# Feed forward of a hybrid decoder layer: seven-product units from the eighth on, with weight sums and low parts moved from VectorE to GpSimd

## The chip, the cores and the metric

The kernel runs on one core of a Trainium2 chip. The metric is the device time of one execution in microseconds; every run named here is a whole execution of the layer.

## What is computed

One inference step of a decoder layer: a mixer (retention and dilated attention), then a SwiGLU feed forward, for a prompt of 512 tokens and 8 sample tokens together (520 columns). Only the feed forward is touched:

```python
def swiglu(xn, w_ffn_in, w_ffn_out):
    a, b = jnp.split(xn @ w_ffn_in, 2, axis=-1)
    return (jax.nn.silu(a) * b) @ w_ffn_out
...
h = h + swiglu(rmsnorm(h, ln2_g[layer]), w_ffn_in[layer], w_ffn_out[layer])
y = rmsnorm(h, lnf_g)
```

The model width is 1024 and the hidden width 2816, which is 22 tiles of 128 (NFF = 22). Everything is float32.

## The kernel before

Columns stand in two halves of 260 (256 prompt tokens and 4 sample tokens). To keep float32 precision each operand of TensorE is split into a high part, rounded by ScalarE, and a low part, which is the difference. A product is then three matmuls: high by high, high by low, low by high. Weights come from memory in subtiles of 128 x 1024 (`load_sub`, 512 KB each, four in flight), and are split in blocks of 128 x 512: `block_hi` (L201) on ScalarE writes `wh`, and two pumps later `low` (L204) on VectorE writes `wl`, five blocks ahead of TensorE (`AHEAD`).

The order is written out by hand. Engines take their instructions in program order. `advance(t)` is called as block t begins on TensorE: it issues the weight sums of blocks up to t + 6 and the high parts of blocks up to t + 5. `pump` is called after every second product of a block: it runs what `later(n, ...)` has put off and advances the generators by one `yield`.

The feed forward is a sequence of units (`FFSEQ`, L29). Unit i makes hidden tile i: a = silu(first product), times b. A plain unit (`ffn_in`) takes 2 x 8 products of 128 x 128 weights for two halves: 96 matmuls, 4 weight blocks. A quad (`ffn_in_quad`) computes the same four quarter results (two outputs by two halves) by the seven products of Winograd's form of Strassen's scheme (`SEVEN`, L284): 7 blocks of 4 x 3 matmuls, 84 in all, but 7 weight blocks, of which three hold sums of weights. `block_sum` makes these on VectorE: L185 two sums in one instruction of 1024 columns, L189 and L191 one each of 512. In a quad, ScalarE copies four of the seven results to SBUF (L313) and VectorE puts results together (`evac`: L1368, L1372, L1376). Two of the three PSUM banks of a quad belong to a pair that the next quad writes again from its first block on.

Output shares (`ffn_out`) are quads too. After a chunk of 8 units, four shares of two output columns each add the chunk's part to hT. Their right factors come from `right` (L1300): for each pair of units (4 tiles of 260 columns, `UF`) it makes four sums on VectorE, and the high parts of seven factors on ScalarE (UH) and their low parts on VectorE (L1318, UL), in three pieces of 780, 520 and 520 columns. It is a generator: pushed by `middle` after the odd unit of a pair, it runs over the pumps of the next unit. For the last chunk (units 16 to 21) `whole` splits each unit's result plainly, and plain products (`LAST` and the loops after it) end the kernel.

The sequence before is: units 0 to 8, four shares, units 9 to 16, four shares, units 17 to 21. Quads are 7, 8, 9, 11, 12, 13, 15, 16, 17, 19, 20, 21; units 10, 14 and 18 are plain. At the end `fin_out` scales the rows and SyncE stores them (L1475, L1477).

GpSimd has no part in the feed forward. Earlier in the kernel it adds the two gated branches (L1146) and sums of squares (L563).

Of the kernel before, what the change touches and what calls it, by code (L numbers as in the profile page):

```python
# [8 lines left out]
F32 = mybir.dt.float32  # L9
F32R = mybir.dt.float32r  # L10
AF = mybir.ActivationFunctionType
ALU = mybir.AluOpType
# [10 lines left out]
NFF = 22  # L23
# [1 line left out]
CHUNKS = ((0, 8), (8, 8), (16, 6))  # L25
LAST = [(c, k) for k0 in (0, 4) for c in range(2) for k in range(k0, min(k0 + 4, 6))]
LAST[8:] = [(0, 4), (1, 4), (0, 5), (1, 5)]
INQ = (7, 8, 9, 11, 12, 13, 15, 16, 17, 19, 20, 21)
FFSEQ = []  # L29
for (a_, n_), ahead_ in zip(CHUNKS, (1, 1, 0)):  # L30
    FFSEQ += [("in", i_, i_ in INQ) for i_ in range(a_ and a_ + 1, a_ + n_ + ahead_)]
    FFSEQ += [("out", c_, True) for c_ in range(0, 8, 2) if ahead_]
QUADS = {128 + 2 * i_: 4 for i_, e_ in enumerate(FFSEQ) if e_[2]}
SCW = (8, 7, 7, 6)
# [4 lines left out]
def tile_hybrid_layer(  # L39
# [9 lines left out]
    V, A, G_, PE, SP = nc.vector, nc.scalar, nc.gpsimd, nc.tensor, nc.sync  # L49
# [13 lines left out]
    def halves(ap):  # L63
        return ap.rearrange("p (f c) -> p f c", f=2)
# [10 lines left out]
    def f32(ap):  # L75
        return ap.bitcast(F32)
# [28 lines left out]
    def later(n, fn):  # L105
        delayed.append([n, fn])
# [31 lines left out]
    def push(name, gen):  # L138
        tracks[name].append(gen)
        return gen  # L140
# [9 lines left out]
    raw, split, qsum = {}, {}, {}  # L150
    blocks, bid = [], {}
    for s_ in range(NSUB):
# [3 lines left out]
        elif s_ - 1 not in QUADS:  # L156
            bid[s_, 0], bid[s_, 1] = len(blocks), len(blocks) + 1
            blocks += [("p", s_, 0), ("p", s_, 1)]
    done = {"add": 0, "hi": 0}
    home = []  # L160

    NRAW = 4
    AHEAD = 5

    def load_sub(s):
        if s < NSUB:
            raw[s] = wpool.tile([128, 1024], F32, tag="raw", bufs=NRAW, name=f"raw{s}")
            SP.dma_start(raw[s], wall[s])

    def left(b):  # L170
        kind, s, j = blocks[b]
        if kind == "p":
            return raw[s][:, 512 * j:512 * j + 512]
        w = 128 * QUADS[s]
        t, i = ((s, 1), ("q", 0), (s + 1, 0), (s + 1, 1), ("q", 1), ("q", 0), (s, 0))[j]
        return (qsum[s] if t == "q" else raw[t])[:, i * w:(i + 1) * w]

    def block_sum(b):
        kind, s, j = blocks[b]
        if kind == "p":  # L180
            return
        w = 128 * QUADS[s]
        if j == 1:
            qsum[s] = home[0].tile([128, 1024], F32, tag="qq", name=f"qq{s}")
            V.tensor_tensor(qsum[s][:, :2 * w].rearrange("p (i c) -> p i c", i=2),  # L185
                            raw[s][:, :2 * w].rearrange("p (i c) -> p i c", i=2),
                            raw[s + 1][:, :w][:, None, :].to_broadcast([128, 2, w]), op=ALU.add)
        elif j == 2:
            V.tensor_tensor(raw[s + 1][:, :w], raw[s][:, w:2 * w], qsum[s][:, :w], op=ALU.add)  # L189
        elif j == 5:  # L190
            V.tensor_tensor(qsum[s][:, :w], raw[s + 1][:, w:2 * w], raw[s + 1][:, :w], op=ALU.add)  # L191

    def block_tiles(b):
        w = 128 * QUADS[blocks[b][1]] if blocks[b][0] == "q" else 512
        split[b] = tuple(wpool.tile([128, 512], F32R, tag=t, bufs=6, name=f"{t}{b}")[:, :w] for t in ("wh", "wl"))
        return split[b]

    def block_hi(b):
        h, l = block_tiles(b)
        r = left(b)  # L200
        A.activation(h, r, AF.Copy)  # L201

        def low():
            V.tensor_tensor(l, r, f32(h), op=ALU.subtract)  # L204
            kind, s, j = blocks[b]
            if kind == "p" and j == 1:
                load_sub(s + NRAW)
            elif kind == "q" and j == 6:
                load_sub(s + NRAW)
                load_sub(s + 1 + NRAW)  # L210

        later(2, low)

    def advance(t):
        while done["add"] < min(t + AHEAD + 2, len(blocks)):
            b = done["add"]
            done["add"] += 1
            block_sum(b)
        while done["hi"] < min(t + AHEAD + 1, len(blocks)):
            b = done["hi"]  # L220
            done["hi"] += 1
            block_hi(b)
# [1045 lines left out]
    UF = {}  # L1268
    NP = CHUNKS[2][0]
    NX = 3  # L1270
# [4 lines left out]
    def whole(i, t):  # L1275
        hi, lo = (halves(u[:, i - NP, :]) for u in (UHp, ULp))
        A.activation(hi, t, AF.Copy)
        later(2, lambda: V.tensor_tensor(lo, t, f32(hi), op=ALU.subtract))

    def middle(i, mult):  # L1280

        if i > NP:
            t = halves(ftmp("fu"))
            mult(t)
            whole(i, t)
            return
        if i % 2 == 0:
            if len(rights) > 1:
                finish("S", rights[-2])
            UF[i // 2] = fp.tile([128, 4, HF], F32, tag="uf", bufs=2, name="uf")  # L1290
        t = UF[i // 2]
        mult(t[:, 1:3, :] if i % 2 else t[:, 0::3, :])
        if i == NX - 1:
            rights.append(push("S", right(UF[0], 0)))
        if i % 2 and i > NX - 1:
            rights.append(push("S", right(t, i % 8 // 2)))

    rights = []

    def right(b, k):  # L1300

        yield
        t = fp.tile([128, 4, HF], F32, tag="us", name="us")
        V.tensor_tensor(t[:, 0, :], b[:, 0, :], b[:, 3, :], op=ALU.subtract)
        yield
        V.scalar_tensor_tensor(t[:, 1, :], b[:, 2, :], -1.0, t[:, 0, :], op0=ALU.mult, op1=ALU.subtract)
        yield
        V.tensor_tensor(t[:, 2, :], b[:, 2, :], b[:, 3, :], op=ALU.subtract)
        yield
        V.scalar_tensor_tensor(t[:, 3, :], t[:, 1, :], -1.0, b[:, 1, :], op0=ALU.mult, op1=ALU.subtract)  # L1310
        yield
        for x, j, n in ((b[:, 0:3], 0, 3), (t[:, 0:2], 3, 2), (t[:, 2:4], 5, 2)):
            hi, lo = (u[:, k, j:j + n, :] for u in (UH4, UL4))
            A.activation(hi, x, AF.Copy)
            yield
            if k < 3:
                yield
            V.tensor_tensor(lo, x, f32(hi), op=ALU.subtract)  # L1318
            if k < 3:
                yield  # L1320

# [60 lines left out]
    def ffn_out(c):  # L1382

        s12, s35 = snaps()
        h1, h2 = halves(hT[:, c, :]), halves(hT[:, c + 1, :])

        def evac(j, bank):
            if j == 3:
                V.tensor_tensor(h1[:, 0, :], bank, h1[:, 0, :], op=ALU.add)
                later(1, lambda: V.tensor_tensor(h1, h1, s12, op=ALU.add))  # L1390
            elif j == 4:
                later(1, lambda: V.tensor_tensor(s35[:, 0, :], s35[:, 0, :], s35[:, 1, :], op=ALU.add))
            elif j == 5:
                V.tensor_tensor(h1[:, 1, :], bank, h1[:, 1, :], op=ALU.add)
                V.tensor_tensor(h2[:, 1, :], h2[:, 1, :], s35[:, 0, :], op=ALU.subtract)
            elif j == 6:
                V.tensor_tensor(h2[:, 0, :], h2[:, 0, :], bank, op=ALU.subtract)

        quad(ufactor, [s12[:, 0, :], s12[:, 1, :], s35[:, 0, :], s35[:, 1, :]], evac)

    for kind, i, seven in FFSEQ:
        if kind == "out":
            if i == 0:
                finish("S", rights[-1])
            ffn_out(i)
            continue
        if i == NP + 1:
            whole(NP, UF[NP // 2][:, 0::3, :])
        (ffn_in_quad if seven else ffn_in)(i)

    last = bpool.tile([128, 7 * D], F32, tag="bg", name="last")
    yt = last[:, :4 * D].rearrange("p (j c) -> p j c", j=4)
# [46 lines left out]
    def fin_out(f):  # L1459
        sq = ftmp("sqf")  # L1460
        A.activation(sq[:, :HF], hT[:, 7, f * HF:(f + 1) * HF], AF.Square)
        fin_ss(f, ssa[:, f * HF:(f + 1) * HF], True)
        a = fin_T(7, f)
        fin_ss(f, sq, False)
        r = rstd_rows(fp, ssb[:, 2 * f:2 * f + 2], 128, 2, D, "nf")
        r4 = rstd_rows(fp, ssb[:4, 4 + f:5 + f], 4, 1, D, "ng")
        fin_g(7, f, *a)
        for i in range(2):
            cs = slice(512 * i, 512 * i + 512)
            for j in (2 * f, 2 * f + 1):  # L1470
                if j % 2:
                    A.activation(yt[:, j, cs], yt[:, j, cs], AF.Copy, scale=r[:, 1:2])
                else:
                    V.tensor_scalar(yt[:, j, cs], yt[:, j, cs], r[:, 0:1], None, op0=ALU.mult)
                SP.dma_start(y_p[0, j * 128:(j + 1) * 128, cs], yt[:, j, cs])  # L1475
        V.tensor_scalar(ys[:, f, :], ys[:, f, :], r4[:4, 0:1], None, op0=ALU.mult)
        SP.dma_start(y_s[4 * f:4 * f + 4].rearrange("r o d -> r (o d)"), ys[:, f, :])  # L1477

# [26 lines left out]
    for f in range(2):  # L1505
        for c in range(4, 8):
            o = free_pair()[:, :1, :]
# [120 lines left out]
```

## Time and profile before

| | us |
|---|---|
| median of 3 runs | 1306.59 |
| lowest and highest of the runs | 1304.96, 1307.02 |
| the profiled execution's own time | 1305.23 |
| its span from first to last instruction | 1303.4 |

PE is TensorE, PEld its weight loads, DVE VectorE, ACT ScalarE, POOL GpSimd, SP SyncE. Times in the trace count from the start of the span. An instruction of VectorE is recorded from its own start, some 0.08 us before the one ahead of it ends, so the price of one in a row of them is the difference of two starts. Matmuls overlap in the records, so their price too is read from starts. Line numbers are those of the code above.

### The profile page before, as it was taken

The page shows a single profiled execution, that of the slowest core. Times are in us where ns is not written, and L with a number is a line of the kernel's source. Part 1 is how long each engine was busy: PE and PEld are TensorE (multiplying, and loading weights), DVE is VectorE, ACT ScalarE, POOL GpSimd, SP SyncE. Part 2 cuts the span into 40 slices and gives each one's busy share as a digit, 9 for nine tenths or more (in the row PEclk, how much of TensorE's full clock was granted, in tenths as well). Part 3 has the DMA queues.
Part 4 walks back from the last instruction along what each step waited for, and adds up shares of the span by engine and source line. Part 5 has one row for each costly group of instructions (what it writes and reads, how often), then busy time and mean ns, then how long its engine had stood idle before and what let it go on. Part 6 is the DMA issues. An engine that isn't in the chain of part 4 may idle for free.

```text
span 1303.4 us, 25688 instructions
## 1 busy us (share of the span) xinstructions
PE 1276.1 (98%) x10465; PEld 1245.0 (96%) x10465; DVE 821.0 (63%) x1737; ACT 573.5 (44%) x1100; POOL 83.6 (6%) x69
## 2 busy tenths in 40 slices
PE   8999999999999999999999999999999999999997
PEld 7999999999898999999999999899999999999997
DVE  7866636847765532234545455476688988798765
ACT  4465334635563522244434343233354555555542
POOL 3601001001002000000000000040000000000000
PEclk8999999999999999999999999999999999999999
DMA  6266344746584332435555545624222333233321
GB/s 213 93 208 230 119 158 140 250 153 230 171 292 149 98 95 84 138 122 159 159 150 157 160 149 189 222 98 147 82 82 82 98 112 100 87 93 113 98 82 66
DMA packets 89782, 183.35 MB, mean 141 GB/s; under 512 B 12024, under 2 KB 33944, under 8 KB 89664
## 3 DMA queue, kind: packets, MB, share of 16 engines
q1 hardware_dynamic: 88944, 180.64, 43.0%
q8 instruction: 82, 1.34, 0.4%
q10 hardware_dynamic: 720, 1.07, 0.3%
q14 instruction: 36, 0.29, 0.1%
HBM read 155.70 MB, written 25.98 MB: 139 GB/s over the span
## 4 chain that ended last, share of the span: by engine, by line
PE 85%; DVE 6%; DMA 3%; issue 2%; ACT 2%; POOL 1%; SPq 1%; DVEq 0%; ACTq 0%
PE pm L251 61%; PE pm L307 10%; PE sp L323 3%; PE pc L307 2%; PE sp L553 2%; DVE wl L204 2%; PE sp L572 1%; DMA vb<-vd 1%; PE pm L1516 1%; PE sp L968 1%; ACT wh L201 1%; PE sp L505 1%; DMA out<-st 1%; PE sp L918 1%; PE sacc L1113 1%
## 5 line engine op out<-in xcount | busy, mean ns | idle before, releaser
L251 PE MATMUL pm<-X,wh 128*128 128x260 f32 x3392 | 560.9, 287 | 4.4 <-DVE X L355 3.6
L251 PEld LDWEIGHTS pm<-X,wh 128*128 128x128 f32 x3392 | 469.5, 189 | 18.9 <-issue 9.1
L204 DVE TENSOR_TENSOR wl<-raw,wh 128x512 fp32r<-128x512 f32 x384 | 274.4, 716 | 165.0 <-ACT wh L201 161.6
L251 PE MATMUL pm<-X,wl 128*128 128x260 f32 x1696 | 342.3, 283 | 0.0
L201 ACT ACTIVATE wh<-raw 128x512 fp32r<-128x512 f32 x384 | 238.7, 625 | 210.7 <-PE pm L251 163.5
L251 PEld LDWEIGHTS pm<-X,wl 128*128 128x128 f32 x1696 | 262.5, 189 | 0.1
L251 PE MATMUL pm<-GA,wh 128*128 128x260 f32 x512 | 82.2, 283 | 0.0
L307 PE MATMUL pm<-XT,wh 128*128 128x260 f32 x384 | 71.5, 285 | 1.4 <-DVE uf L1376 1.2
L251 PE MATMUL pm<-XP,wh 128*128 128x260 f32 x448 | 71.9, 283 | 0.0
L251 PEld LDWEIGHTS pm<-GA,wh 128*128 128x128 f32 x512 | 70.1, 188 | 0.0
L307 PEld LDWEIGHTS pm<-XT,wh 128*128 128x128 f32 x384 | 59.1, 188 | 3.0 <-DVE uf L1376 2.0
L251 PEld LDWEIGHTS pm<-XP,wh 128*128 128x128 f32 x448 | 61.3, 188 | 0.0
L307 PE MATMUL pm<-UH,wh 128*128 128x260 f32 x192 | 54.6, 284 | 3.9 <-DVE fa L1368 2.8
L332 POOL TENSOR_TENSOR r<-v,cst 128x4 f32<-128x4 f32 (+4 forms) x14 | 17.6, 1261 | 598.0 <-DVE v L330 598.0
L307 PE MATMUL pm<-UH,wl 128*128 128x260 f32 x192 | 54.3, 283 | 0.0
L307 PE MATMUL pm<-UL,wh 128*128 128x260 f32 x192 | 54.3, 283 | 0.0
L307 PE MATMUL pm<-XT,wl 128*128 128x260 f32 x192 | 54.1, 282 | 0.0
L658 DVE SCALAR_TENSOR_TENSOR st<-st,kv 128x512 f32<-128x512 f32 x64 | 45.5, 714 | 13.3 <-ACT kv L623 11.5
L623 ACT ACTIVATE kv<-vb,ks 128x512 f32<-128x512 f32 x64 | 44.0, 714 | 22.0 <-DMA vb<-vd 20.8
L251 PE MATMUL pm<-GA,wl 128*128 128x260 f32 x256 | 51.6, 283 | 0.0
L313 ACT ACTIVATE s<-pm 128x260 f32<-128x260 f32 x80 | 30.9, 387 | 46.7 <-PE pm L307 46.4
L201 ACT ACTIVATE wh<-qq 128x512 fp32r<-128x512 f32 x60 | 37.0, 626 | 24.2 <-PE pm L251 11.6
(324 smaller groups left out, 2097.0 us busy)
## 6 DMA issues: line engine op xcount, KB each, us to landing
raw<-wall SPq DMA_DIRECT2D x192, 512.0 KB
st<-state SPq DMA_DIRECT2D x64, 256.0 KB
out<-st SPq DMA_DIRECT2D x64, 256.0 KB
area<-ck SPq DMA_DIRECT2D x24, 512.0 KB
vb<-vd SPq DMA_DIRECT2D x32, 256.0 KB
area<-qd SPq DMA_DIRECT2D x12, 512.0 KB
cb<-cd SPq DMA_DIRECT2D x4, 768.0 KB
xr<-xT SPq DMA_DIRECT2D x8, 260.0 KB
```

The source lines that it names most:

```text
L201: A.activation(h, r, AF.Copy)
L204: V.tensor_tensor(l, r, f32(h), op=ALU.subtract)
L251: PE.matmul(pm[:, f, :HF], w, x[f] if isinstance(x, tuple) else x[:, f * HF:(f + 1) * HF], start=first, stop=last)
L307: PE.matmul(out[bank], w[:, ks], factor(i, k, x), start=bank not in begun, stop=k == nkp - 1 and w is l, skip_group_check=True)
L313: A.activation(snap[(0, 3, 1, None, 2)[j]], out[bank], AF.Copy)
L323: PE.transpose(out, in_, ident[:n, :n])
L332: G_.tensor_tensor(r[:rows, :ncol], v[:rows, :ncol], mhalf[:rows].to_broadcast([rows, ncol]), op=ALU.pow)
L505: PE.matmul(sp[:, :T - i0], x[:, dt, jb * 128:(jb + 1) * 128], y[:, dt, i0:], start=i == 0, stop=i == len(mm) - 1)
L553: PE.matmul(sp[:, i0:], v[x][:, jb, c * 128:(c + 1) * 128], scs[y][:, SCO[jb]:SCO[jb] + T - i0], start=jb == 0 and x == y, stop=jb == 3 an ...
L572: PE.matmul(sp, kt[x][:, jb, dt * 128:(dt + 1) * 128], v[y][:, jb, :], start=jb == 0 and x == y, stop=jb == 3 and x == 1)
L623: A.activation(kvs[i][:, :DV], vbs[b], AF.Copy, scale=ks[:, dt, b:b + 1])
L658: V.scalar_tensor_tensor(sts[i], sts[i], GAMMA[h], kvs.pop(i)[:, :DV], op0=ALU.mult, op1=ALU.add)
```

## The change

`INQ` becomes all units from 7 on, and each run of output shares begins two units after its chunk's last unit instead of one: units 0 to 9, shares, 10 to 17, shares, 18 to 21. The first weight sum of a quad is made by GpSimd, two blocks earlier than before and into a tile of two buffers; VectorE makes the next two in place, block 2; GpSimd makes the fourth. The low parts in `right` are made by GpSimd. The `right` of the pair that was finished ahead of the shares (8 and 9) is pushed behind them, and so is `whole` for units 16 and 17. In the last `fin_out` the odd rows' stores are issued by ScalarE.

```diff
-INQ = (7, 8, 9, 11, 12, 13, 15, 16, 17, 19, 20, 21)
+INQ = tuple(range(7, NFF))
...
-    FFSEQ += [("in", i_, i_ in INQ) for i_ in range(a_ and a_ + 1, a_ + n_ + ahead_)]
+    FFSEQ += [("in", i_, i_ in INQ) for i_ in range(a_ and a_ + 2, min(a_ + n_ + 2, NFF))]
...
-        t, i = ((s, 1), ("q", 0), (s + 1, 0), (s + 1, 1), ("q", 1), ("q", 0), (s, 0))[j]
+        t, i = ((s, 1), ("q", 0), (s + 1, 0), (s + 1, 1), (s, 1), ("q", 0), (s, 0))[j]
...
+    def block_first_sum(b):
+
+        kind, s, j = blocks[b]
+        if kind == "q" and j == 0:
+            w = 128 * QUADS[s]
+            qsum[s] = home[0].tile([128, 512], F32, tag="qq", bufs=2, name=f"qq{s}")
+            G_.tensor_tensor(qsum[s][:, :w], raw[s][:, :w], raw[s + 1][:, :w], op=ALU.add)
...
-        if j == 1:
-            qsum[s] = home[0].tile([128, 1024], F32, tag="qq", name=f"qq{s}")
-            V.tensor_tensor(qsum[s][:, :2 * w].rearrange("p (i c) -> p i c", i=2),
-                            raw[s][:, :2 * w].rearrange("p (i c) -> p i c", i=2),
-                            raw[s + 1][:, :w][:, None, :].to_broadcast([128, 2, w]), op=ALU.add)
-        elif j == 2:
-            V.tensor_tensor(raw[s + 1][:, :w], raw[s][:, w:2 * w], qsum[s][:, :w], op=ALU.add)
-        elif j == 5:
-            V.tensor_tensor(qsum[s][:, :w], raw[s + 1][:, w:2 * w], raw[s + 1][:, :w], op=ALU.add)
+        if j == 2:
+            assert (s, 0) in lowered
+            V.tensor_tensor(raw[s][:, w:2 * w], raw[s][:, w:2 * w], raw[s + 1][:, :w], op=ALU.add)
+            V.tensor_tensor(raw[s + 1][:, :w], raw[s][:, :w], raw[s][:, w:2 * w], op=ALU.add)
+        elif j == 4:
+            assert (s, 1) in lowered
+            G_.tensor_tensor(qsum[s][:, :w], raw[s + 1][:, w:2 * w], raw[s + 1][:, :w], op=ALU.add)
...
+        while done["first"] < min(t + AHEAD + 4, len(blocks)):
+            b = done["first"]
+            done["first"] += 1
+            block_first_sum(b)
...
-        if i > NP:
+        if i > NP + 1:
...
-        if i % 2 and i > NX - 1:
+        if i % 2 and i > NX - 1 and i not in FIRSTS:
             rights.append(push("S", right(t, i % 8 // 2)))
...
+    FIRSTS = (9, 17)
...
-            V.tensor_tensor(lo, x, f32(hi), op=ALU.subtract)
+            G_.tensor_tensor(lo, x, f32(hi), op=ALU.subtract)
...
             ffn_out(i)
+            if i == 6:
+                o = FIRSTS[n_out]
+                n_out += 1
+                if o > NP:
+                    whole(NP, UF[NP // 2][:, 0::3, :])
+                    whole(NP + 1, UF[NP // 2][:, 1:3, :])
+                else:
+                    rights.append(push("S", right(UF[o // 2], 0)))
             continue
-        if i == NP + 1:
-            whole(NP, UF[NP // 2][:, 0::3, :])
...
-                SP.dma_start(y_p[0, j * 128:(j + 1) * 128, cs], yt[:, j, cs])
+                (A if f and j % 2 else SP).dma_start(y_p[0, j * 128:(j + 1) * 128, cs], yt[:, j, cs])
```

## Rows read from the trace of the kernel before

**Rows 1.** The page, part 1: busy time, share of the span, instructions of each engine.

```profile
PE 1276.1 (98%) x10465; PEld 1245.0 (96%) x10465; DVE 821.0 (63%) x1737; ACT 573.5 (44%) x1100; POOL 83.6 (6%) x69
```

**Rows 2.** The chain of waits in order of time: start us, us, what.

```profile
1006.44 4.31 PE pm L307 x36
...
1035.07 8.65 PE pm L307 x72
...
1045.16 8.65 PE pm L307 x72
...
1079.73 11.49 PE pm L251 x96
...
1124.16 11.49 PE pm L251 x96
...
1135.64 4.31 PE pm L307 x36
...
1208.94 11.49 PE pm L251 x96
```

**Rows 3.** The waits of TensorE from 880 us on: total us, times, longest.

```profile
PE pm L307 <- DVE fa L1368: 3.6, 3, 1.4
PE pm L307 <- DVE uf L1376: 2.3, 3, 1.2
```

**Rows 4.** The timeline of VectorE in unit 12: start us, us, instruction [idle before].

```profile
1105.27 1.22 DVE L185 TENSOR_TENSOR qq<-raw,raw 128x1024 f32<-128x1024 f32 x1
1106.40 0.43 DVE L1310 SCALAR_TENSOR_TENSOR us<-us,uf 128x260 f32<-128x260 f32 x1
...
1107.35 0.68 DVE L189 TENSOR_TENSOR raw<-raw,qq 128x512 f32<-128x512 f32 x1
1107.95 0.68 DVE L204 TENSOR_TENSOR wl<-qq,wh 128x512 fp32r<-128x512 f32 x1
1108.55 0.96 DVE L1318 TENSOR_TENSOR UL<-uf,UH 128x780 fp32r<-128x780 f32 x1
1109.43 0.42 DVE L1368 TENSOR_TENSOR fa<-pc,s 128x260 f32<-128x260 f32 x1
...
1111.92 0.42 DVE L1368 TENSOR_TENSOR fa<-pm,s 128x260 f32<-128x260 f32 x1
1112.26 0.68 DVE L191 TENSOR_TENSOR qq<-raw 128x512 f32<-128x512 f32 x1
1113.57 0.69 DVE L204 TENSOR_TENSOR wl<-qq,wh 128x512 fp32r<-128x512 f32 x1 [0.63 <-ACT wh L201]
1114.18 0.69 DVE L1318 TENSOR_TENSOR UL<-us,UH 128x520 fp32r<-128x520 f32 x1
1114.79 0.42 DVE L1376 SCALAR_TENSOR_TENSOR uf<-pm,fa 128x260 f32<-128x260 f32 x1
```

**Rows 5.** The timelines of VectorE (three rows) and GpSimd (one) after 859 us.

```profile
859.67 0.69 DVE L1148 TENSOR_TENSOR M<-sgat,M 128x520 fp32r<-128x520 f32 x1
860.28 1.80 DVE L204 TENSOR_TENSOR wl<-raw,wh 128x512 fp32r<-128x512 f32 x1
862.01 0.68 DVE L1145 TENSOR_TENSOR sgbt<-sgbt,pm 128x520 f32<-128x520 f32 x1
...
859.84 1.70 POOL L1146 TENSOR_TENSOR sgat<-sgat,sgbt 128x520 f32<-128x520 f32 x1 [1.17 <-DVE sgbt L1145]
```

**Rows 6.** The timelines of VectorE and GpSimd after 301 us, one row each.

```profile
301.15 0.75 DVE L564 SCALAR_TENSOR_TENSOR GT<-sp,vec,g 128x512 f32<-128x512 f32 x1 [2.60 <-ACT sq L562]
...
301.26 1.30 POOL L563 TENSOR_TENSOR ssa<-ssa,sq 128x512 f32<-128x512 f32 x1 [2.06 <-ACT sq L562]
```

**Rows 7.** Windows: stretch, length, busy us of PE, PEld, DVE, ACT, POOL, clock, DMA.

```profile
1091.20:1101.40 10.20, 10.20 (x88) 10.20 (x87) 8.00 (x13) 5.71 (x12) 0.00 (x0) 1.00 0.20 63
1030.50:1070.80 40.30, 40.30 (x335) 40.30 (x336) 37.06 (x66) 21.63 (x43) 0.00 (x0) 1.00 0.32 102
```

**Rows 8.** The timeline of SyncE's queue at the end.

```profile
1298.03 1.81 SPq L1475 DMA_DIRECT2D out<-last  x4
```

More of the change, by code (lines that the diff above doesn't have):

```diff
@@ L158, in tile_hybrid_layer @@
             blocks += [("p", s_, 0), ("p", s_, 1)]
-    done = {"add": 0, "hi": 0}
+    done = {"first": 0, "add": 0, "hi": 0}
     home = []
@@ L174, in left @@
         w = 128 * QUADS[s]
-        t, i = ((s, 1), ("q", 0), (s + 1, 0), (s + 1, 1), ("q", 1), ("q", 0), (s, 0))[j]
+        t, i = ((s, 1), ("q", 0), (s + 1, 0), (s + 1, 1), (s, 1), ("q", 0), (s, 0))[j]
         return (qsum[s] if t == "q" else raw[t])[:, i * w:(i + 1) * w]
+    lowered = set()
+    def block_first_sum(b):
[4 more added lines that the diff above has]
+            G_.tensor_tensor(qsum[s][:, :w], raw[s][:, :w], raw[s + 1][:, :w], op=ALU.add)
     def block_sum(b):
@@ L205, in low @@
             kind, s, j = blocks[b]
+            lowered.add((s, j))
             if kind == "p" and j == 1:
@@ L1399, in ffn_out @@
         quad(ufactor, [s12[:, 0, :], s12[:, 1, :], s35[:, 0, :], s35[:, 1, :]], evac)
+    n_out = 0
     for kind, i, seven in FFSEQ:
```

## The prediction

> **What bounds the kernel now.** I read the page first: TensorE is busy for 98% of the span, VectorE for 63%, GpSimd for 6% [rows 1]. So a microsecond is won only by giving TensorE less to do or by removing the places where it waits. Next, the chain of waits gives the length of the pieces. A plain feed-forward unit (96 products) takes 11.49 us, and an output share of seven products, 84 of them, takes 1045.16 - 1035.07 = 10.09 us when nothing holds it [rows 2]. The same rows show where TensorE is held. From 1006.44 to 1079.73 lie seven quads (units 7 and 8, four output shares, unit 9): 73.29 us against 7 x 10.09 = 70.63, so 2.66 lost. From 1135.64 to 1208.94 lie seven more (15, 16, four shares, 17): 2.67 lost. Units 11, 12 and 13 run from 1079.73 + 11.49 = 1091.22 to 1124.16, 32.94 against 30.27: 2.67 lost. Together 8.0 us. The waits of TensorE name the releaser: VectorE's additions of L1368 and its products of L1376, three times each [rows 3]. Both empty a bank that the next block writes.
>
> VectorE's timeline in unit 12 says why [rows 4]. A generator `right` makes seven right factors from each pair of units; it advances one step per pump, and a quad has 14 pumps, so all of it falls into the even unit that follows the pair. Starts of neighbours give the true price of one instruction: 0.60 us for 512 columns (1107.35 to 1107.95), 0.61 for 520 (1114.18 to 1114.79), 0.88 for 780 (1108.55 to 1109.43), 0.34 for 260 (1111.92 to 1112.26), 1.13 for 1024 (1105.27 to 1106.40). VectorE's work in an even quad is 7 low parts, 4.20; sums 1.13 + 0.60 + 0.60 = 2.33; five emptyings of 260, 1.70; `right` 4 x 0.34 + 0.88 + 2 x 0.61 = 3.46. That is 11.69 us against 10.09. The odd quad, without `right`, is 8.23. Units 10, 14 and 18 are plain now, and two of them absorb a `right`; units 8, 12 and 16 do not, and lose 2.67 each.
>
> **The change, part by part.**
>
> (a) Units 10, 14 and 18 become quads: 3 x (11.49 - 10.09) = 4.2 us less on TensorE, and that is on the path.
>
> (b) Weight sums. VectorE loses the 1024-wide sum and one of 512 and gains one of 512: -1.13 us per quad. GpSimd gets two of 512.
>
> (c) Low parts of the right factors: VectorE loses 0.88 + 0.61 + 0.61 = 2.10 per pair; GpSimd gets 780 and twice 520 columns.
>
> Without contention, (b) and (c) would settle the matter: the even quad would ask 8.46 us of VectorE and every wait would go. But the trace shows what a GpSimd addition does beside VectorE [rows 5]. GpSimd's addition of 520 columns begins at 859.84. VectorE finishes M, and its next instruction, a low part with two operands in SBUF, takes 1.80 us instead of 0.69. From the start of M to the start after the low part VectorE spends 862.01 - 859.67 = 2.34, of which 0.61 and 0.60 are its own: 1.13 us went to GpSimd. The pattern repeats for every M. By contrast an instruction of VectorE that takes one operand from PSUM runs beside a GpSimd addition undelayed, 0.75 us [rows 6]. So I price a GpSimd addition of 512 or 520 columns at 1.13 us of VectorE, and 780 columns in proportion at 1.70; it is hidden where VectorE is idle or works from PSUM. GpSimd's own record says 1.70 us for the 520 [rows 5]; if the whole of it blocked, a pair would lose another 4 us.
> The Trainium skill bears on that choice: Perfetto Trace Analysis, section GPSIMD Engine Instruction, says that a GpSimd span in a profile is not to be trusted and that spacing of starts is the better measure. By that rule, too, the smaller price stands.
> No row shows GpSimd writing the rounded type that `right` needs. VectorE's own price does not depend on it (sum and low part are both 0.60 in [rows 4]), so I take none; the bound above is the 1.70 of the record, below it is no block at all.
>
> Now unit by unit. An even quad up to its second L1368 loses 1.13 - 0.60 = 0.53 of sums and two low parts, 0.88 + 0.61 = 1.49: 2.02 less. In that stretch GpSimd runs the 780 low part, the fourth sum of the next quad and the first sum of the one after: 1.70 + 1.13 + 1.13 = 3.96 more. Of this I take 0.8 as hidden: VectorE has one idle place of 0.63 [rows 4], and one instruction in six reads PSUM, five chances at 0.34/6 each, 0.3. So VectorE reaches that point 1.1 later. Behind it the sum of L191 (0.60) and a low part (0.61) fall away, and one GpSimd low part (1.13) comes in: -0.1. An even quad then loses 2.67 + 1.0 = 3.7 us. The third low part slips into the odd quad, where VectorE is busy 8.00 us now [rows 7]: 8.00 - 1.13 + 3 x 1.13 = 10.3 at worst, nothing lost to speak of.
>
> Even quads with a `right` beside them were three and are five: 8, 10, 12, 14, 16. So 5 x 3.7 = 18.5 lost, where 8.0 were: +10.5.
>
> (d) Output shares two units later. A `right` no longer ends just ahead of them; it still ends in an even quad, so the wait moves from the start of the shares to units 8 and 16 and is in the five. In a share VectorE is busy 37.06/4 = 9.27 us [rows 7]; 9.27 - 1.13 + 2.26 = 10.4 less up to 1.0 for three instructions that read PSUM: 9.4 to 10.4 against 10.09. I take nothing; the upper end is 8 x 0.3 = 2.4.
>
> (e) `right` of units 8 and 9 starts after the shares, in unit 10; `whole` of 16 and 17 in unit 18, 2 x 0.61 of VectorE in a quad without `right`: nothing. The first weight sum is issued two blocks earlier and may wait for its weights at the head of GpSimd's queue; behind it stand only low parts that no block needs soon.
>
> (f) At the end two of five stores are issued by ScalarE, not SyncE, whose four row stores take 1.81 us in a row [rows 8]. The bytes are the same; the first is issued as before. Between -0.5 and +0.3; I take 0.
>
> Sum: -4.2 + 10.5 = +6.3. The profiled execution took 1305.2 us (span 1303.4), so it would take 1311.5. The median of the runs is 1306.6, 1.4 above it, and I carry the difference over: **1313 us**. Differences under 0.2% (2.6 us) are what a measurement of this kernel cannot tell from none.
>
> **The rivals.**
>
> *GpSimd fits into VectorE's gaps (faster).* If only the 780 low part and one sum meet VectorE before the emptying, the stretch is 1.70 + 1.13 - 0.8 - 2.02 = 0 later, and behind it 1.2 is saved with nothing coming in: an even quad loses 1.5, five lose 7.5, and the result is -0.5 - 4.2 = -4.7: 1302. For it: VectorE is idle 2.2 us of the odd quad [rows 7], and GpSimd is free to run when its operands are there. Against: GpSimd was started by the very stretch of VectorE work it collides with in [rows 5]. Without any contention all 8.0 would go, 1294.4; the trace speaks against that in every repetition. The Trainium skill (SBUF — State Buffer, section Who interferes with whom) frees only those instructions of VectorE that take at most one input from SBUF; [rows 6] agrees, and by that rule this rival would need most of VectorE's work to come from PSUM, which it does not.
>
> *A draw.* Even quads at 2.0 to 3.0 us: 10 to 15 lost, so -2.2 to +2.8: 1304.4 to 1309.4.
>
> *GpSimd becomes the bound (slower still).* Place: the in-place sum of block 2, which VectorE may write only after GpSimd has read the same columns for its first sum. GpSimd has 1.70 + 4 x 1.13 = 6.2 us of blocked time per even quad, by its record 4 x 1.70 and half as much again for the 780, 9.4 of 10.09. It decides once GpSimd is a block (1.44) behind: then VectorE stands still with the emptyings queued behind the sum. All five additions ahead of the emptying would give 1.70 + 4 x 1.13 - 0.8 - 2.02 - 1.2 = 2.2 more per even quad, 4.9 lost, 24.5 in all, and with 2.4 in the shares: +16.5 + 2.4 - 4.2 = +14.7, 1321.
>
> **How the numbers follow.** My forecast, 1309.5 to 1317, has 0.45; GpSimd as the bound 0.12; a draw 0.20; faster 0.23. Left out of the range are the unblocked case and the worst of the backlog: 1302 to 1320. Slower by over 0.2% is 0.57. The forecast's own range is 1309.5 to 1317.
>
> **What the profile would show.** Right: TensorE with 36 products fewer; GpSimd with some 6 us of additions per even quad; many low parts of VectorE at 1.2 to 1.8 us instead of 0.69 in units 7 to 21; TensorE's waits behind L1368 and L1376 once for each of units 8, 10, 12, 14, 16, some 3 to 4 us each, and none at the first output share. Wrong: low parts that stay at 0.69 beside GpSimd, waits of TensorE below 9 us in total, or waits that end on GpSimd rather than VectorE.

## The result and the profile after

The change is slower: 1356.76 us, median of 4 runs (1354.37 to 1359.3), against 1305.78 us of the kernel before on the same chip (1302.91 to 1307.02): ratio 1.0394, 95% interval 1.0366 to 1.0422. The profiled execution took 1354.37 us with a span of 1352.6, that is 49.2 more than the span before.

The page of the changed kernel, part 1, beside [rows 1]:

```profile
PE 1283.2 (95%) x10429; PEld 1243.8 (92%) x10429; DVE 866.6 (64%) x1720; ACT 580.0 (43%) x1121; POOL 197.2 (15%) x139
```

TensorE has its 36 instructions fewer. VectorE has 17 instructions fewer and is 45.6 us longer busy.

Line numbers from here on are those of the kernel that is being read. In the changed kernel L320 is L307 of the kernel before, L326 is L313, L209 is L201, L212 is L204, L1382 is L1368 and L1390 is L1376; L1408 adds a PSUM result to hT in a share.

The waits of TensorE from 1000 us on, beside [rows 3] (line waited for: total us, times, longest):

```profile
PE pm L320 <- DVE fa L1382: 22.0, 13, 3.2
PE pm L320 <- DVE hT L1408: 12.4, 8, 1.6
PE pm L320 <- DVE uf L1390: 5.3, 10, 0.6
PE pm L320 <- ACT s L326: 5.0, 5, 1.3
PE pm L320 <- DVE fu L1390: 1.6, 3, 0.6
```

Before there were six such waits, 5.9 us, all behind units. Now there are 39, 46.3 us. Every output share (`hT`, eight times) and every unit from 7 on but the last has one. In the waits of all engines from 1000 to 1300 us GpSimd is not named once as the one waited for.

The chain of waits of the changed kernel in order of time (start us, us, what), three shares and then the fourth blocks of units 10, 12 and 14, beside [rows 2]:

```profile
1060.67 4.59 PE pm L320 x36
...
1072.57 4.59 PE pm L320 x36
...
1084.46 4.59 PE pm L320 x36
...
1115.62 1.43 PE pc L320 x12
...
1142.72 1.43 PE pc L320 x12
...
1169.81 1.43 PE pc L320 x12
```

A share takes 11.9 us instead of 10.09, a pair of units 27.1 instead of 2 x 10.09 = 20.2.

The timeline of VectorE in one share (start us, us, instruction, idle time before it), then GpSimd's:

```profile
1075.30 0.69 DVE L212 TENSOR_TENSOR wl<-raw,wh 128x512 fp32r<-128x512 f32 x1 [0.91 <-ACT wh L209]
1076.68 0.69 DVE L212 TENSOR_TENSOR wl<-raw,wh 128x512 fp32r<-128x512 f32 x1 [0.70 <-ACT wh L209]
...
1079.42 0.42 DVE L1403 TENSOR_TENSOR hT<-pc,hT 128x260 f32<-128x260 f32 x1
1079.88 1.55 DVE L1404 TENSOR_TENSOR hT<-hT,s 128x520 f32<-128x520 f32 x1
1081.35 1.77 DVE L212 TENSOR_TENSOR wl<-raw,wh 128x512 fp32r<-128x512 f32 x1
1083.05 0.41 DVE L1406 TENSOR_TENSOR s<-s 128x260 f32<-128x260 f32 x1
1083.39 0.68 DVE L212 TENSOR_TENSOR wl<-raw,wh 128x512 fp32r<-128x512 f32 x1
1083.99 0.42 DVE L1408 TENSOR_TENSOR hT<-pm,hT 128x260 f32<-128x260 f32 x1
```

```profile
1079.58 1.29 POOL L199 TENSOR_TENSOR qq<-raw 128x512 f32<-128x512 f32 x1 [8.90 <-DVE wl L212]
1080.82 1.75 POOL L186 TENSOR_TENSOR qq<-raw,raw 128x512 f32<-128x512 f32 x1
```

GpSimd idles 8.9 us, until the low part of block 1 is made. Then it runs the fourth sum and right behind it the first sum of the quad after next. VectorE alternates with it: L1404 takes 1.55 us (0.70 unblocked, in the kernel with fills below), the low part 1.77 (0.69 unblocked). Some 2 us later than it would have, VectorE reaches L1408, the emptying of a bank that TensorE waits for. Some 4 us earlier VectorE had stood idle for 0.91 and 0.70 us.

The same two timelines in unit 12, an even unit with a `right`:

```profile
1128.20 2.32 DVE L195 TENSOR_TENSOR raw<-raw,raw 128x512 f32<-128x512 f32 x1
...
1132.18 1.64 DVE L212 TENSOR_TENSOR wl<-raw,wh 128x512 fp32r<-128x512 f32 x1
1133.74 1.53 DVE L1386 TENSOR_TENSOR s<-s 128x260 f32<-128x260 f32 x1
1135.20 1.74 DVE L212 TENSOR_TENSOR wl<-raw,wh 128x512 fp32r<-128x512 f32 x1
1136.86 0.42 DVE L1382 TENSOR_TENSOR fa<-pm,s 128x260 f32<-128x260 f32 x1
```

```profile
1128.09 1.89 POOL L1332 TENSOR_TENSOR UL<-uf,UH 128x780 fp32r<-128x780 f32 x1 [7.04 <-ACT UH L1328]
1132.01 1.26 POOL L199 TENSOR_TENSOR qq<-raw 128x512 f32<-128x512 f32 x1 [2.03 <-DVE wl L212]
1133.23 1.75 POOL L1332 TENSOR_TENSOR UL<-us,UH 128x520 fp32r<-128x520 f32 x1
1134.95 1.45 POOL L186 TENSOR_TENSOR qq<-raw,raw 128x512 f32<-128x512 f32 x1
```

Four additions of GpSimd stand ahead of L1382, and each meets a VectorE instruction: 1.63 us on L195 (2.32 against 0.69), then 0.95 on a low part, 1.1 on L1386 and 1.05 on the next low part.

### The profile page after: what moved, and what is told of

The parts are those of the page before. It is cut to its first block, busy times and chain, and to the rows that moved or that the text cites. A ratio compares the mean times of both kernels' runs of the same rounds, so it can differ in the third digit from the quotient of the medians.

```text
span 1352.6 us, 25785 instructions
## 1 busy us (share of the span) xinstructions
PE 1283.2 (95%) x10429; PEld 1243.8 (92%) x10429; DVE 866.6 (64%) x1720; ACT 580.0 (43%) x1121; POOL 197.2 (15%) x139
## 4 chain that ended last, share of the span: by engine, by line
PE 75%; DVE 13%; issue 5%; DMA 4%; ACT 2%; POOL 1%; SPq 1%; ACTq 0%; DVEq 0%
PE pm L264 53%; PE pm L320 9%; DVE wl L212 4%; PE sp L336 3%; PE sp L566 2%; PE pc L320 2%; DMA vb<-vd 2%; DVE s L1386 1%; PE sp L585 1%; PE pm L1537 1%; PE sp L981 1%; DMA out<-st 1%; DVE raw L195 1%; ACT wh L209 1%; PE sp L518 1%
## 5 line engine op out<-in xcount | busy, mean ns | idle before, releaser
L212 DVE TENSOR_TENSOR wl<-raw,wh 128x512 fp32r<-128x512 f32 x407 | 321.4, 792 | 178.5 <-ACT wh L209 176.7
L209 ACT ACTIVATE wh<-raw 128x512 fp32r<-128x512 f32 x407 | 253.0, 625 | 227.6 <-PE pm L264 153.1
L320 PE MATMUL pm<-XT,wh 128*128 128x260 f32 x480 | 92.9, 292 | 11.3 <-ACT s L326 5.0
L320 PEld LDWEIGHTS pm<-XT,wh 128*128 128x128 f32 x480 | 75.9, 194 | 15.6 <-ACT s L326 7.0
L320 PE MATMUL pm<-XP,wh 128*128 128x260 f32 x240 | 47.2, 295 | 23.4 <-DVE fa L1382 20.3
L320 PE MATMUL pm<-XT,wl 128*128 128x260 f32 x240 | 68.7, 286 | 0.0
L320 PE MATMUL pm<-UH,wh 128*128 128x260 f32 x192 | 55.2, 287 | 12.0 <-DVE hT L1408 9.3
L326 ACT ACTIVATE s<-pm 128x260 f32<-128x260 f32 x92 | 35.4, 385 | 62.9 <-PE pm L320 59.0
L320 PEld LDWEIGHTS pm<-XP,wh 128*128 128x128 f32 x240 | 37.8, 193 | 26.2 <-DVE fa L1382 22.6
L320 PE MATMUL pm<-UL,wh 128*128 128x260 f32 x192 | 54.3, 283 | 0.0
L320 PE MATMUL pm<-UH,wl 128*128 128x260 f32 x192 | 54.3, 283 | 0.0
L199 POOL TENSOR_TENSOR qq<-raw 128x512 f32<-128x512 f32 x23 | 29.8, 1296 | 153.5 <-DVE wl L212 153.5
```

What stands on the lines that cost most here:

```text
L199: G_.tensor_tensor(qsum[s][:, :w], raw[s + 1][:, w:2 * w], raw[s + 1][:, :w], op=ALU.add)
L320: PE.matmul(out[bank], w[:, ks], factor(i, k, x), start=bank not in begun, stop=k == nkp - 1 and w is l, skip_group_check=True)
L326: A.activation(snap[(0, 3, 1, None, 2)[j]], out[bank], AF.Copy)
```

## The experiments

Two things had to be told apart: whether GpSimd's additions cause the loss at all or the new order of the units does, and, if they do, whether it is how much they block or where the block falls. The period of a share is read from one row per kernel: all instructions of the last subtraction of a share (L1397 before, L1411 in the change) in the first four shares, with the first and the last start; their distance is three periods. The rows of the kernel before and of the change:

```profile
L1397 DVE TENSOR_TENSOR hT<-hT,pm x4: 418/419/419, 1040.0 to 1070.3; 128x260 f32<-128x260 f32 x4
```

```profile
L1411 DVE TENSOR_TENSOR hT<-hT,pm x4: 410/412/414, 1061.5 to 1097.2; 128x260 f32<-128x260 f32 x4
```

They give 10.1 and 11.9 us. Each kernel was timed beside the kernel before, whose medians on the chips used were 1302.8 to 1305.8 us; the ratios take that out, a difference between the medians of two experiments does not. Where units are named below, the period is the distance of the first matmuls of neighbouring quads' fourth blocks (`pc`) in the timeline. Before, an even quad so measured takes 12.55 us and an odd one 10.33; in the change 14.7 to 17.8 and 12.1.

**All on VectorE.**

```diff
-G_.tensor_tensor(qsum[s][:, :w], raw[s][:, :w], raw[s + 1][:, :w], op=ALU.add)
+V.tensor_tensor(qsum[s][:, :w], raw[s][:, :w], raw[s + 1][:, :w], op=ALU.add)
...
-G_.tensor_tensor(qsum[s][:, :w], raw[s + 1][:, w:2 * w], raw[s + 1][:, :w], op=ALU.add)
+V.tensor_tensor(qsum[s][:, :w], raw[s + 1][:, w:2 * w], raw[s + 1][:, :w], op=ALU.add)
...
-G_.tensor_tensor(lo, x, f32(hi), op=ALU.subtract)
+V.tensor_tensor(lo, x, f32(hi), op=ALU.subtract)
...
-while done["first"] < min(t + AHEAD + 4, len(blocks)):
+while done["first"] < min(t + AHEAD + 1, len(blocks)):
```

> The changed kernel with every weight sum and low part back on VectorE; the order of the units, all seven-product units from 7 on and the later shares stay. (The first sum is issued three blocks later than in the change, where the kernel before had it, and into one buffer.) Theory A, GpSimd's additions block VectorE: with none of them output shares come back to 10.1 us and odd units to 10.1 to 10.4 us; VectorE still has 11.7 us of work in each of the five even units, so these stay at some 12.7 us: 1297 to 1312 us in all. Theory B, it is the new order and the lack of plain units that overloads VectorE, whoever adds: shares and odd units stay near 12 us and the total is over 1335 us.

Measured: 1318.37 us, ratio 1.0104 (1.0089 to 1.0119). Shares 10.5 us, odd units 10.55, even units 13.2 to 14.5.

```profile
L1411 DVE TENSOR_TENSOR hT<-hT,pm x4: 415/416/417, 1052.4 to 1083.9; 128x260 f32<-128x260 f32 x4
```

VectorE with 70 additions more to do is faster than VectorE with GpSimd's help: 38 us of the 51 go. Theory B falls. The total is 6 us over the top of the expectation; the kernel with the old sums, below, shows where that comes from.

**The low parts alone, and the sums alone, on GpSimd.** The first kernel keeps `G_` in the low parts' line only, the second in the two sums' lines only (there with the change's own lead and buffers).

> As the first kernel of this set, but the low parts of the right factors are GpSimd's, as in the change; all weight sums are VectorE's. Theory A: shares at 10.1 us and odd units near 10.3 us, since no GpSimd work falls there; even units at 13 to 14.5 us, the two with the dense generator at 14 to 16 us; total 1310 to 1325 us. Theory B: over 1335 us.

> The changed kernel with only the low parts of the right factors back on VectorE; the two weight sums stay with GpSimd. Theory A: the two sums start together as soon as the low part of block 1 is ready, always between the third and the last but one emptying, and put that emptying off by two blocks of 1.1 us: shares stay at 11.9 us, odd units at 12.1 us, even units at 13.5 to 15 us; total 1335 to 1348 us, so that most of the loss is the sums' and not the low parts'. Theory C, it is the amount of blocked time that counts, wherever it falls: shares, where VectorE has the least work, near 10.1 to 10.4 us, and a total of 1310 to 1325 us.

Measured: low parts alone 1329.99 us, ratio 1.0187 (1.0170 to 1.0204), shares 10.5, odd units 10.56, even 15.1 to 16.3. Sums alone 1349.22 us, ratio 1.0337 (1.0322 to 1.0352), shares 11.9, odd units 12.1, even 14.0 to 15.3:

```profile
L1411 DVE TENSOR_TENSOR hT<-hT,pm x4: 407/409/413, 1060.6 to 1096.3; 128x260 f32<-128x260 f32 x4
```

So the low parts act only in the even units, as forecast, and cost 11.6 us over the kernel with all on VectorE. They cost more there than expected: even units and the total (5 us over the top) lie above their ranges. The sums act in every quad and carry most of the loss: with them alone the kernel is within 8 us of the change, and 1 us over the top of what was expected. Theory C falls in the shares.

**All on VectorE, the generator over two units.** Each `yield` of `right` is doubled.

```diff
             A.activation(hi, x, AF.Copy)
             yield
-            if k < 3:
-                yield
+            yield
+            yield
+            yield
...
             yield
+            yield
```

> As the first kernel of this set, all on VectorE, with the generator of the right factors stretched over the 28 pumps of two units instead of 14. If an even unit is late only because VectorE has 11.7 us of work there and 8.3 us in the odd one, both come to about 10.1 to 10.6 us: 1290 to 1300 us, faster than the kernel before. If it is some chain through ScalarE in every unit that is late, nothing changes against the first kernel.

Measured: 1311.95 us, ratio 1.0057 (1.0042 to 1.0072), 6.4 us under the kernel without the stretch and 12 over the top of what was expected. Odd and even units are level now, at 11.2 to 11.5 us: VectorE's uneven load was real, but something else held every unit. The kernels with the old sums, below, point to the place of the fourth sum.

**Additions that nobody needs.** To the kernel with all on VectorE, at the low part of block 1:

```diff
+            if kind == "q" and j == 1:
+                scr = home[0].tile([128, 512], F32, tag="scr", name=f"scr{b}")
+                for _ in range(2):
+                    G_.tensor_tensor(scr, f32(h), f32(l), op=ALU.add)
```

and, in the second kernel, fills in their place:

```diff
-                for _ in range(2):
-                    G_.tensor_tensor(scr, f32(h), f32(l), op=ALU.add)
+                G_.tensor_tensor(scr[:, :8], f32(h[:, :8]), f32(l[:, :8]), op=ALU.add)
+                for _ in range(4):
+                    G_.memset(scr, 0.0)
```

> The kernel with everything on VectorE, and beside it two GpSimd additions of 512 columns for each quad whose results nobody uses, started by the same event as the change's two sums (the low part of block 1). No engine waits for their results. Theory A, blocked reads: shares go from 10.1 to 11.9 us, every odd unit to about 12 us, and the total is 35 to 50 us over the kernel without the additions. Theory D, the change lost by waiting for GpSimd's results: nothing changes by more than 2 us.

> As the kernel with the unused additions, but GpSimd, started by the same event through one addition of 8 columns, only writes: four fills of 512 columns of about 0.5 us each. If what blocks VectorE is GpSimd's reading, shares stay at 10.1 to 10.3 us and the total within 4 us of the kernel with everything on VectorE. If any GpSimd work on SBUF blocks VectorE, shares go to 11.9 us as with the additions.

Measured: with the additions 1376.96 us, ratio 1.0563 (1.0528 to 1.0597); with the fills 1319.83 us, ratio 1.0124 (1.0082 to 1.0166), against 1318.37 without either. GpSimd in the two kernels, in one share each:

```profile
1082.61 3.00 POOL L218 TENSOR_TENSOR scr<-wh,wl 128x512 f32<-128x512 f32 x2 [9.50 <-DVE wl L212]
```

```profile
1067.78 0.20 POOL L217 TENSOR_TENSOR scr<-wh,wl 128x8 f32<-128x8 f32 x1 [7.95 <-DVE wl L212]
1068.05 2.28 POOL L219 MEMSET scr<- 128x512 f32 x4
```

VectorE's next instructions, the addition of 520 columns of a share and the low part behind it, first beside the additions, then the addition beside the fills:

```profile
1082.84 1.63 DVE L1408 TENSOR_TENSOR hT<-hT,s 128x520 f32<-128x520 f32 x1
1084.39 1.77 DVE L212 TENSOR_TENSOR wl<-raw,wh 128x512 fp32r<-128x512 f32 x1
```

```profile
1068.01 0.70 DVE L1409 TENSOR_TENSOR hT<-hT,s 128x520 f32<-128x520 f32 x1
```

No engine waits for `scr` in the trace, so theory D falls: the block alone is enough, and costs 57.1 us against the kernel with fills on the same chip, more than the 35 to 50 expected. (Shares went to 12.5 and 14.0 us, over the 11.9 expected: here VectorE also has the fourth sum ahead of the emptying, and some stretches ran at a lower clock, 0.72 of full speed from 1086 to 1092 us; more on that in the last section.) The fills, 2.28 us in a row, change nothing that can be measured; shares take 10.5 us as without them. The Trainium skill (SBUF — State Buffer, section Who interferes with whom) has it that a GpSimd instruction which only writes does not contend with a VectorE instruction of two SBUF inputs; this run agrees, 0.70 us beside 1.63.

**The new order alone.** The change with `left`, `block_sum` and the low parts as in the kernel before, all on VectorE.

> The new order of the units alone: all units from 7 on as quads, shares two units later, the stores of the end; weight sums and low parts exactly as in the kernel before, on VectorE. Shares back to 10.1 us (the first kernel with everything on VectorE had 10.48, since its fourth sum stands ahead of the last emptyings), odd units 10.3 us, even units 12.5 us: the three plain units gained 4.2 us, two more late even units lose 4.9 us: 1302 to 1308 us, no change against the kernel before.

Measured: 1307.43 us, ratio 1.0009 (0.9995 to 1.0023): no difference. Shares 10.1 us, odd units 10.33, the five even units 12.25 to 12.55, as expected. It is 10.9 us faster than the first experiment, which differs from it in the arrangement of the sums alone. The timelines of VectorE in a share show one difference ahead of an emptying that TensorE waits for, in the first experiment and then here (L1408 there is L1395 here):

```profile
1070.55 0.68 DVE L199 TENSOR_TENSOR qq<-raw 128x512 f32<-128x512 f32 x1
...
1072.09 0.42 DVE L1408 TENSOR_TENSOR hT<-pm,hT 128x260 f32<-128x260 f32 x1
```

```profile
1069.52 0.42 DVE L1395 TENSOR_TENSOR hT<-pm,hT 128x260 f32<-128x260 f32 x1
...
1070.20 0.69 DVE L191 TENSOR_TENSOR qq<-raw 128x512 f32<-128x512 f32 x1
```

With in-place sums on VectorE, the fourth sum stands ahead of that emptying and not behind it; a share that takes 10.1 here takes 10.5 there, a unit of the last chunk 10.7 here and 11.0 to 11.4 there. The arrangement of the sums was the extra of the first experiment, and by the same reading, which was not tested by itself, of the fourth.

**More room in PSUM, by halves.** In `quad`, two tiles are held and their two halves are used in turn; made from the change, from the kernel with the new order alone, and from that with the stretched generator.

```diff
-        pms = {}
-        for _ in range(2):
-            i = turn["next"]
-            pms[i] = bank_pair(i)[:, 0, :HF]
+        if not held:
+            for _ in range(2):
+                i = turn["next"]
+                held[i] = bank_pair(i)
+            held["half"] = 1
+        held["half"] ^= 1
+        pms = {i: held[i][:, held["half"], :HF] for i in range(2)}
```

> The change as it stands, GpSimd's additions at their places, but successive quads use the two halves of their PSUM tiles in turn (a quad uses one half of each; the other stood empty), so a quad's last emptyings are due one quad later. Theory P, the place: the two sums cost 1.8 us in a share only because they fall just ahead of an emptying that TensorE is about to wait for; with a quad of room shares run at 10.1 to 10.5 us, and odd and even units together at 22 to 23.5 us a pair: 1302 to 1318 us. Theory Q, the amount: VectorE is full with what GpSimd blocks, wherever it falls: shares stay at 11.5 us or more and the total over 1335 us.

> The kernel with the new order alone, and successive quads in the two halves of their PSUM tiles in turn. VectorE has 11.7 us of work in an even unit and 8.2 us in an odd one, 19.9 us for a pair against 20.2 us of TensorE; with one quad of room TensorE should hardly wait: pairs at 20.2 to 21 us, 1290 to 1297 us in all, faster than the kernel before. If a chain through ScalarE holds each unit and not the banks, 1300 us or more.

> The same with the generator of the right factors stretched over two units as well. Pairs at 20.2 to 20.5 us: 1289 to 1296 us. If the banks alone already give all there is, no difference against the kernel without the stretch.

Measured: from the change 1358.26 us, ratio 1.0413 (1.0383 to 1.0442), as the change; from the new order alone 1307.18 us, ratio 1.0018 (1.0007 to 1.0030), as without, where 1290 to 1297 had been expected. TensorE's waits of the first:

```profile
PE pm L325 <- DVE hT L1413: 12.4, 8, 1.6
```

They are those of the change, 12.4 us in 8 times: the halves did not take the wait away, so this edit decided nothing between P and Q. Why they gave no room was not found out. The third, with the generator stretched, took 1298.13 us, ratio 0.9945 (0.9926 to 0.9964): 2 us over the top of its range, but faster than the kernel before and than the new order alone. All its quads up to the second run of shares take 10.06 to 10.49 us, and of the waits of TensorE behind VectorE in quads 0.5 us is left:

```profile
PE pm L312 <- DVE uf L1388: 0.5, 3, 0.2
```

Since the halves change nothing in the other two, the gain most likely belongs to the even load of VectorE; that is not shown, because the stretch without the halves was not run on these sums.

**The same GpSimd work, one sum later.**

```diff
-            qsum[s] = home[0].tile([128, 512], F32, tag="qq", bufs=2, name=f"qq{s}")
+            qsum[s] = home[0].tile([128, 512], F32, tag="qq", name=f"qq{s}")
...
-        while done["first"] < min(t + AHEAD + 4, len(blocks)):
+        while done["first"] < min(t + AHEAD + 1, len(blocks)):
```

> The change with one thing moved: GpSimd's first weight sum is issued three blocks later, into one buffer, so that it starts after the last low part of the quad before has been made, in the first blocks of a quad, where VectorE now idles; the fourth sum and the low parts stay. GpSimd does exactly as much. Theory P, the place: of the 1.8 us that a share loses, the part of one addition, some 1.1 us, goes: shares at 10.5 to 10.9 us, odd units likewise near 11 us: 1320 to 1335 us. Theory Q, the amount: shares stay at 11.9 us and the total at 1350 us or more.

(The change issues this sum three blocks ahead of the kernel before, not two as the description of the change and part (e) have it: `advance` reached six blocks ahead for a sum made with block 1 of a quad, and reaches eight ahead for one made with block 0.)

Measured: 1342.87 us, ratio 1.0287 (1.0262 to 1.0311); shares 10.8 us, odd units 11.0, even units 16.2 to 16.9. GpSimd's first sum in a share, and VectorE's low part beside it:

```profile
1082.29 1.29 POOL L186 TENSOR_TENSOR qq<-raw,raw 128x512 f32<-128x512 f32 x1 [4.40 <-DVE wl L212]
```

```profile
1083.12 1.00 DVE L212 TENSOR_TENSOR wl<-raw,wh 128x512 fp32r<-128x512 f32 x1 [0.91 <-ACT wh L209]
```

The first sum now falls where VectorE idles, and blocks one low part by 0.3 us instead of 1.1. The shares and odd units do what theory P said. The total is 8 us above its range: units 10, 12 and 14 lose 1.6 to 1.9 us more than in the change (units 8 and 16 less), and TensorE's waits for ScalarE's copies rise from 5.0 to 12.0 us; what the sum meets there, beside the work of `right`, was not followed.

**More room in PSUM, by other tiles.** From the change:

```diff
+        held[0] ^= 1
+        if held[0]:
+            pms = {i: sbank("qs")[:, :HF] for i in range(2)}
+        else:
+            pms = {}
+            for _ in range(2):
+                i = turn["next"]
+                pms[i] = bank_pair(i)[:, 0, :HF]
```

> The change as it stands, but every second quad uses two other PSUM tiles (those of the side work, which are free in this stretch); halves of one tile had not taken the waits away, since they still named the same additions as their releaser. Now a quad's last emptyings are due one quad later. Theory P: shares at 10.1 to 10.5 us and pairs of units at 22 to 24 us: 1300 to 1322 us. Theory Q: no share under 11.5 us, total over 1340 us.

Measured: 1334.75 us, ratio 1.0218 (1.0201 to 1.0235). The last subtraction of two shares, two periods apart in the first four, and TensorE's waits:

```profile
L1416 DVE TENSOR_TENSOR hT<-hT,qs x2: 413/414/416, 1061.3 to 1081.5; 128x260 f32<-128x260 f32 x2
```

```profile
PE qs L325 <- ACT s L331: 19.9, 11, 4.2
PE pm L325 <- ACT s L331: 6.8, 5, 3.3
```

Shares are back at 10.1 us, odd units at 10.4 to 10.8, though GpSimd blocks VectorE as before. In shares and odd units the loss was the place, not the amount. Even units stay at 15.1 to 16.7 us, unit 18 takes 15.4, and TensorE now waits for ScalarE's copies. In unit 12 such a copy (L331) stands behind a split that waits 4.14 us for VectorE's in-place sum (L196), and ahead of that sum VectorE has an addition of 260 columns that GpSimd's 780 block, 2.12 us instead of 0.42:

```profile
1119.77 1.94 POOL L1337 TENSOR_TENSOR UL<-uf,UH 128x780 fp32r<-128x780 f32 x1 [5.65 <-ACT UH L1333]
...
1119.87 2.12 DVE L1327 TENSOR_TENSOR us<-uf 128x260 f32<-128x260 f32 x1
...
1124.63 0.63 ACT L209 ACTIVATE wh<-raw 128x512 fp32r<-128x512 f32 x1 [4.14 <-DVE raw L196]
...
1125.69 0.37 ACT L331 ACTIVATE s<-qs 128x260 f32<-128x260 f32 x1
```

So in this even unit the blocked time reaches TensorE by way of ScalarE's queue. Whether the place or the amount decides there is not shown. The total lies between the two expectations, for that reason.

## Why the prediction was right and wrong

The direction was right, and so were the mechanism, that an addition of GpSimd blocks VectorE, and its price. An addition takes 1.13 us from VectorE for 512 or 520 columns by [rows 5]; in the change it took 0.85 to 1.1, and 1.63 for 780, forecast at 1.70. That no price was set for the rounded type was right as well. Part (a), 36 products, came as forecast, and the new order alone made 1307.4 us: the three quads' gain of 4.2 us and two more late even units, at 2.46 each, cancel.

The size was wrong: +51 against +6.3, far outside 1302 to 1320. By the `pc` periods the quads from unit 7 on lose 61.6 us against 10.09 each; the same measure gives 9.3 in the kernel before. The parts:

| | forecast lost | measured lost |
|---|---|---|
| intervals with the end of one of the five even units | 18.5 | 29.0 |
| the 14 other intervals up to unit 18: odd units and shares | 0 | 26.4 |
| units 18 to 21 (3 intervals) | 0 | 6.2 |

61.6 - 9.3 less the 4.2 of part (a) is 48.1 of the 49.2 us; most of the rest, 0.8 us, lies ahead of the first quad's fourth block, where a plain unit already waits 1.1 us for a VectorE that GpSimd had blocked.

**The step that failed is the handling of shares and odd quads, in part (d) and in the count "unit by unit".** I put VectorE's work and the blocked time of a quad in one sum, 9.4 to 10.4 us in a share and 10.3 in an odd quad against 10.09, and took nothing, with 8 x 0.3 = 2.4 as the upper end for the shares and "nothing lost to speak of" for the odd quads. The sum was about right: there VectorE does have the time. But GpSimd's two sums are set off by one event, the low part of block 1, and so land on the VectorE instructions just ahead of an emptying that TensorE waits for. In the share shown they block VectorE for 1.9 us; each of the fourteen intervals lost 1.8 to 2.05. That the sums on GpSimd alone keep shares at 11.9, that unused additions at the same event do as much or more, and that the same work with one sum later or with room in PSUM brings them to 10.8 and 10.1, shows it. The prediction looked for deadlines in the even quad and for totals in the others. Units 18 to 21, which the forecast's sum leaves out, lost 6.2 us by the same kind of wait. None of the three signs of being wrong appeared, because they ask after the price and the engine waited for, and not after the place.

**A second term was too small, the even quad.** I counted three additions ahead of the second emptying and hid 0.8 us of them. Unit 12 shows four of the five, and none hidden: 1.63 + 0.95 + 1.1 + 1.05 = 4.7 us where 3.16 stood. Units 10, 12 and 14 lose 4.6 to 4.9 us, units 8 and 16 7.7 and 7.0, with `right` at its denser pace there and the clock lowered behind the wait. This is the rival "all additions ahead of the emptying" (4.9 per even quad); I gave it 0.12, and its place, the in-place sum waiting until GpSimd has read its columns, was not what made it so: TensorE's waits end on VectorE's L1382, and no engine waits for GpSimd. That its 4.9 came so near is in part luck: it has five additions and 0.8 us of them hidden, the trace four and none hidden.

Part (d) said the waits at the first share would go, since `right` no longer ends ahead of them; the new order alone shows that (10.35 us into the first share against 12.55 before). In the change itself the first share still begins with two waits, 0.72 and 0.55 us. Parts (e) and (f) were not tested by themselves.

## What to carry to other kernels

An addition moved from a busy in-order engine to a helper that blocks it is not priced by adding up engine time: ask which event starts it and which of the first engine's instructions stands next. Here a block ahead of an emptying was paid in full, and one in an idle place cost far less. Before moving work, try to spread it: the new order with every sum left on VectorE as before, one generator stretched over two units and PSUM used by halves, which alone changed nothing, won 0.55%. And test a theory of contention with work whose result nobody needs.

## What the runs showed of the hardware that was not expected

TensorE's clock fell after long waits within the feed forward. In the change (windows: stretch, length, busy us of PE, PEld, DVE, ACT, POOL, granted clock, DMA share, GB/s):

```profile
1030.00:1036.00 6.00, 2.77 (x17) 2.56 (x16) 4.78 (x6) 1.68 (x3) 2.95 (x2) 0.78 0.17 34
1035.00:1040.00 5.00, 5.00 (x25) 5.00 (x24) 2.66 (x5) 1.96 (x5) 0.00 (x0) 0.50 0.34 107
```

TensorE was busy 2.77 of 6 us, with one wait of 3.23 us, and from 1035 to 1040 us the granted clock was 0.50 of full speed: 1.2 GHz instead of 2.4. In the chain of waits this is one piece:

```profile
1034.24 7.25 PE pm L320 x36
```

36 products took 7.25 us where [rows 2] have 4.31 for 36. It happened behind unit 8 and again behind unit 16, the two with the longest waits (3.23 us each), and not behind the waits of 2.65 us in units 10, 12 and 14. So a wait of TensorE can cost more than its length. The length alone does not decide it: in the kernel with all on VectorE the clock fell to 0.50 behind unit 8 after a wait of 2.31 us, and not behind unit 16 after one of 2.32.
